# Moving a 56 KB result store from ScalarE's queue amid the loads to SyncE's queue behind the last loads

## Chip, cores, metric

One core of a Trainium2 chip. The metric is the device time of one execution in microseconds (us), the median of several. The kernel before takes 162.1 us.

## The reference

```python
def setup_inputs():
    batch, seq, dim = 32, 512, 1024
    return {"x": np.random.randn(batch, seq, dim).astype(np.float32)}

def reference(x):
    return np.sum(x, axis=-1).astype(np.float32)
```

So 16384 rows of 1024 floats, 67.1 MB read, and 64 KB written. The kernel can hardly be faster than its loads.

## The kernel before

Each of the 128 partitions holds 112 rows of the first block and 16 of the second. Rows come in tiles of 16 a partition (8 MB), three buffers deep, all loaded on SyncE's queue. VectorE sums them; ScalarE helps with seven rows of the last full-width tile and with half of the final block. The final block is loaded in pieces of 9, 4, 2 rows and one row cut at column 544, so that little work is left when the last bytes land. The part that the change touches:

```python
    for b, n in enumerate(BLOCKS):                 # BLOCKS = (112, 16)
        x_b, out_b, res = block(done * P, n)
        ...
        while c < whole:
            ...                                    # loads of 16 rows on nc.sync, sums
            rows_dve(xt, res, 0, m - a, c)
            rows_act(xt, res, m - a, a, c + m - a)
            c += m
        if not final:
            for i, k in ((0, 104), (104, P)):
                nc.scalar.dma_start(out=out_b[i:k], in_=res[i:k])
        done += n

    xt = xpool.tile([P, G * D], F32, tag="xt", name="xt")
    cuts = [0, 9, 13, 15]
    for i, k in zip(cuts, cuts[1:]):
        nc.sync.dma_start(out=xt[:, i * D : k * D], in_=x_b[:, (c + i) * D : (c + k) * D])
    last = 15 * D
    for i, k in ((0, CUT), (CUT, D)):
        nc.sync.dma_start(...)                     # the last row in two pieces
    ...                                            # sums of the final block, VectorE and ScalarE
    nc.sync.dma_start(out=out_b, in_=res)          # the final store, 16 columns
```

Of the kernel before, what the change touches and what calls it, by code (L numbers as in the profile page):

```python
# [1 line left out]

# [4 lines left out]

F32 = mybir.dt.float32
ADD = mybir.AluOpType.add
COPY = mybir.ActivationFunctionType.Copy  # L10
X = mybir.AxisListType.X

BLOCKS = (112, 16)
G = 16
ACT_ROWS = 7
CUT = 544
EARLY = 2


@with_exitstack  # L20
def row_sums(
    ctx: ExitStack,
    tc: tile.TileContext,
    x: bass.AP,
    out: bass.AP,
):
    nc = tc.nc
    P = nc.NUM_PARTITIONS

    x_flat = x.flatten_outer_dims()  # L30
    R, D = x_flat.shape
    C = R // P
    assert R % P == 0 and sum(BLOCKS) == C
    out_flat = out.rearrange("a (b c) -> (a b c)", c=1)

    xpool = ctx.enter_context(tc.tile_pool(name="x", bufs=3))
    rpool = ctx.enter_context(tc.tile_pool(name="res", bufs=1))
    part = rpool.tile([P, 1], F32, name="part")
    seen = rpool.tile([P, 1], F32, name="seen")
    pairs = [rpool.tile([P, D // 2], F32, name=f"pairs{i}") for i in range(3)]  # L40

    def rows_dve(xt, res, j, n, c):
        nc.vector.tensor_reduce(  # L43
            out=res[:, c : c + n],
            in_=xt[:, j * D : (j + n) * D].rearrange("p (j d) -> p j d", d=D),
            axis=X,
            op=ADD,
        )

    def sum_act(v, acc):  # L50
        nc.scalar.activation(out=v, in_=v, func=COPY, accum_out=acc)  # L51

    def rows_act(xt, res, j, n, c):
        for i in range(n):
            sum_act(xt[:, (j + i) * D : (j + i + 1) * D], res[:, c + i : c + i + 1])

    def pairs_dve(xt, a, b, first, acc, pairs):
        h = (a + b) // 2
        nc.vector.tensor_tensor_reduce(  # L59
            out=pairs[:, 0 : h - a], in0=xt[:, a:h], in1=xt[:, h:b], scale=1.0, scalar=first,  # L60
            op0=ADD, op1=ADD, accum_out=acc,
        )

    def block(r0, n):
        x_b = x_flat[r0 : r0 + P * n].rearrange("(p c) d -> p (c d)", p=P)
        out_b = out_flat[r0 : r0 + P * n].rearrange("(p c) -> p c", p=P)
        return x_b, out_b, rpool.tile([P, n], F32, name=f"res{r0}")

    full = C - G
    done = 0  # L70
    for b, n in enumerate(BLOCKS):
        x_b, out_b, res = block(done * P, n)
        final = b == len(BLOCKS) - 1
        whole = n - G if final else n
        c = 0
        while c < whole:
            m = min(G, whole - c)
            xt = xpool.tile([P, G * D], F32, tag="xt", name="xt")
            parts = (0, 1, m) if done + c == 0 else (0, m)
            for i, k in zip(parts, parts[1:]):  # L80
                nc.sync.dma_start(
                    out=xt[:, i * D : k * D], in_=x_b[:, (c + i) * D : (c + k) * D]
                )
            a = ACT_ROWS if done + c + m == full else 0
            rows_dve(xt, res, 0, m - a, c)
            rows_act(xt, res, m - a, a, c + m - a)
            c += m
        if not final:

            for i, k in ((0, 104), (104, P)):  # L90
                nc.scalar.dma_start(out=out_b[i:k], in_=res[i:k])
        done += n

    xt = xpool.tile([P, G * D], F32, tag="xt", name="xt")
# [5 lines that stand above are left out]
        nc.sync.dma_start(  # L100
            out=xt[:, last + i : last + k],
            in_=x_b[:, c * D + last + i : c * D + last + k],
        )

    for i, k in zip(cuts[:2], cuts[1:3]):
        h = (k - i) // 2
        rows_dve(xt, res, i, h, c + i)
        rows_act(xt, res, i + h, k - i - h, c + i + h)
    pairs_dve(xt, 13 * D, 14 * D, 0.0, res[:, c + 13 : c + 14], pairs[2])
    rows_act(xt, res, 14, 1, c + 14)  # L110
    pairs_dve(xt, last, last + CUT, 0.0, part, pairs[0])


    nc.vector.tensor_copy(out=seen, in_=part)  # L114
    pairs_dve(xt, last + CUT, last + D, part, res[:, c + 15 : c + 16], pairs[1])
    nc.sync.dma_start(out=out_b, in_=res)


def kernel(tc: tile.TileContext, x: bass.AP, out: bass.AP):
    row_sums(tc, x, out)  # L120
    tc.close()
    tc.compile()  # L122



    sp = mybir.EngineType.SP
    fn = tc.nc.m.functions[0]
    entry, body = None, None
    for blk in fn.blocks:
        ops = [i for i in blk.instructions if i.engine == sp]  # L130
        if entry is None:
            entry = blk
        elif any(i.opcode == "DMACopy" for i in ops):
            body = blk
            break
    code = list(body.instructions)
    loads = [i for i in code if i.engine == sp][:EARLY]
    for load in loads:
        assert load.opcode == "DMACopy" and not load.sync_info.on_wait
        code.remove(load)  # L140
    body.instructions = code
    code = list(entry.instructions)
    at = next(k for k, i in enumerate(code) if i.engine == sp and i.opcode == "Drain")
    code[at:at] = loads
    entry.instructions = code

# [1 line left out]
_INS = ['x']  # L148
_OUTS = [((32, 512), 'float32')]


# [23 lines left out]
```

## Time and profile before

| | before |
|---|---|
| median time, first 3 runs | 162.1 us (162.03 to 162.14) |
| span of the profiled run | 160.6 us |
| VectorE, ScalarE busy | 76%, 11% of the span |
| load queue (q1) | 97.2% of 16 DMA engines |
| last load piece landed, final store issued, final store landed | 157.80, 158.36, 159.78 us |

Three kinds of reading are used below. The page gives shares. The list in order of time gives start and length of each instruction; a wait stands in brackets behind it. And the trace also keeps a record of each DMA packet (start, length, queue, bytes) and of each semaphore update. Those records do not name the DMA engine, but its packets follow each other end to start within some 5 ns, so an engine can be followed through its long packets. Packet times that no profile line shows are read from those records.

### The profile page before, as it was taken

How to read it: one execution, taken by the hardware profiler on the slowest of the kernel's cores; microseconds unless marked ns; L12 is line 12 of the kernel's file. 1: busy time of each engine (PE TensorE's matmuls, PEld its weight loads, DVE VectorE, ACT ScalarE, POOL GpSimd, SP SyncE). 2: the span in 40 equal slices, each digit the busy share in tenths (PEclk: the TensorE clock that was granted, in tenths of full speed). 3: DMA queues.
4: the chain of work that ended last, by engine and by line, in shares of the span. 5: the costliest groups of instructions: out<-in, count | busy, mean ns of one | idle time of the engine just before them, and what ended most of it. 6: DMA issues, size and time to landing. Idle time of an engine off the chain costs nothing.

```text
span 160.6 us, 120 instructions
## 1 busy us (share of the span) xinstructions
DVE 121.4 (76%) x16; ACT 17.2 (11%) x31; POOL 0.2 (0%) x4
## 2 busy tenths in 40 slices
DVE  0000059997799958999499994999949999598884
ACT  0000000000000000000000000000000000596892
POOL 0000000000000000000000000000000000000000
DMA  9997996996996996996996979979969969998991
GB/s 375 490 398 337 490 522 294 490 522 261 522 506 278 522 506 278 522 506 278 522 506 278 522 326 457 522 310 473 522 294 490 522 261 522 432 432 369 410 402 62
DMA packets 2169, 67.18 MB, mean 418 GB/s; under 512 B 505, under 2 KB 633, under 8 KB 889
## 3 DMA queue, kind: packets, MB, share of 16 engines
q1 hardware_dynamic: 2016, 67.12, 97.2%
q10 hardware_dynamic: 153, 0.06, 0.1%
HBM read 67.11 MB, written 0.07 MB: 418 GB/s over the span
## 4 chain that ended last, share of the span: by engine, by line
DMA 75%; DVE 22%; SPq 0%; issue 0%; DVEq 0%
DMA xt<-in_x_dram 75%; DVE res L43 21%; DVE pairs L59 1%; SPq L97 0%; DVE seen L114 0%; DVE part L59 0%; DVEq L122 0%; DVE res L59 0%
## 5 line engine op out<-in xcount | busy, mean ns | idle before, releaser
L43 DVE TENSOR_REDUCE res<-xt 128x16 f32<-128x16384 f32 (+3 forms) x9 | 119.8, 13309 | 36.6 <-DMA xt<-in_x_dram 36.6
L51 ACT ACT_TABLE_LOAD x1 | 1.3, 1283 | 138.3 <-DMA xt<-in_x_dram 138.3
L51 ACT ACTIVATE xt<-xt 128x1024 f32<-128x1024 f32 x15 | 15.6, 1042 | 2.2 <-DMA xt<-in_x_dram 2.2
L51 ACT ACTIVATION_READ_ACCUMULATOR xt<-xt 128x1 f32 x15 | 2.8, 186 | 0.0
L59 DVE CUSTOM_DVE_ANT_0 pairs<-xt 128x512 f32<-128x512 f32 (+1 forms) x2 | 1.1, 566 | 0.3 <-DMA xt<-in_x_dram 0.3
L59 DVE CUSTOM_DVE_ANT_0 pairs<-xt,part 128x240 f32<-128x240 f32 x1 | 0.5, 467 | 0.0
L114 DVE COPY seen<-part 128x1 f32<-128x1 f32 x1 | 0.2, 153 | 0.0
L59 DVE DVE_READ_ACCUMULATOR2_ANT res<- 128x1 f32 x2 | 0.2, 81 | 0.0
L159 POOL MEMSET const-bfloat16-1.0<- 128x1 bf16 x1 | 0.1, 101 | 0.0
L159 POOL MEMSET const-uint8-127<- 128x1 uint8 x1 | 0.1, 101 | 0.0
L159 POOL MEMSET const-float32-0.0<- 128x1 f32 x1 | 0.1, 98 | 0.2 <-issue 0.2
L159 POOL MEMSET const-float32-1.0<- 128x1 f32 x1 | 0.1, 98 | 0.0
L59 DVE DVE_READ_ACCUMULATOR2_ANT part<- 128x1 f32 x1 | 0.1, 84 | 0.0
## 6 DMA issues: line engine op xcount, KB each, us to landing
xt<-in_x_dram SPq DMA_DIRECT2D x1, 7680.0 KB
xt<-in_x_dram SPq DMA_DIRECT2D x1, 4608.0 KB, 32.4
xt<-in_x_dram SPq DMA_DIRECT2D x1, 2048.0 KB, 36.9
xt<-in_x_dram SPq DMA_DIRECT2D x1, 1024.0 KB, 39.0
xt<-in_x_dram SPq DMA_DIRECT2D x1, 512.0 KB, 3.9
xt<-in_x_dram SPq DMA_DIRECT2D x1, 272.0 KB, 39.1
xt<-in_x_dram SPq DMA_DIRECT2D x1, 240.0 KB, 38.9
xt<-in_x_dram SPq DMA_DIRECT2D x6, 40.9
```

The lines of the kernel that those rows point to most:

```text
L43: nc.vector.tensor_reduce(out=res[:, c : c + n], in_=xt[:, j * D : (j + n) * D].rearrange("p (j d) -> p j d", d=D), axis=X, op=ADD,)
L51: nc.scalar.activation(out=v, in_=v, func=COPY, accum_out=acc)
L59: nc.vector.tensor_tensor_reduce(out=pairs[:, 0 : h - a], in0=xt[:, a:h], in1=xt[:, h:b], scale=1.0, scalar=first, op0=ADD, op1=ADD, accum ...
L114: nc.vector.tensor_copy(out=seen, in_=part)
L159: nc = _bacc.Bacc("TRN2", target_bir_lowering=False, num_devices=1)
```

## The change

The intent: keep the store's packets out of the way of the last loads, by queuing them behind these on the same queue, so that they run while VectorE finishes the last sums.

```diff
         if not final:
-            for i, k in ((0, 104), (104, P)):
-                nc.scalar.dma_start(out=out_b[i:k], in_=res[i:k])
+            out_a, res_a = out_b, res
         done += n
 ...
+    for i, k in ((0, 64), (64, P)):              # behind the loads of the final block
+        nc.sync.dma_start(out=out_a[i:k], in_=res_a[i:k])
```

Three things change at once: the queue, the place behind the loads, and the split.

## The prediction

> **What bounds the kernel now.** I read the page of the profile first (busy shares, chain that ended last), then the chain in order of time, the order-of-time list of the last microseconds, and then the DMA queues in narrow stretches around the moment when the store moves. From the page and its DMA part:
>
> ```profile
> span 160.6 us, 120 instructions
> DVE 121.4 (76%) x16; ACT 17.2 (11%) x31; POOL 0.2 (0%) x4
> DMA packets 2169, 67.18 MB, mean 418 GB/s; under 512 B 505, under 2 KB 633, under 8 KB 889
> q1 hardware_dynamic: 2016, 67.12, 97.2%
> q10 hardware_dynamic: 153, 0.06, 0.1%
> DMA 75%; DVE 22%; SPq 0%; issue 0%; DVEq 0%
> ```
>
> The reader should see that the load queue (q1, SyncE's) fills 97.2% of the time of 16 DMA engines, while VectorE is busy for 76% and ScalarE for 11%. The kernel reads 67.11 MB and the DMA engines are never idle until the end; the chain's 22% on VectorE is time in which loads run beside it (it holds a buffer, the next loads are already queued). So the time is: start-up, the stream of loads, and a short tail after the last bytes land. Only these can change it. ScalarE's queue (q10, which carries the store that the change moves) has 0.1%.
>
> The tail, from the list in order of time of the last four microseconds:
>
> ```profile
> 156.62 0.69 DVE L59 CUSTOM_DVE_ANT_0 pairs<-xt 128x512 f32<-128x512 f32 x1 [0.26 <-DMA xt<-in_x_dram]
> 157.24 0.44 DVE L59 CUSTOM_DVE_ANT_0 pairs<-xt 128x272 f32<-128x272 f32 x1
> 157.73 0.15 DVE L114 COPY seen<-part 128x1 f32<-128x1 f32 x1
> 157.82 0.47 DVE L59 CUSTOM_DVE_ANT_0 pairs<-xt,part 128x240 f32<-128x240 f32 x1
> 158.36 0.35 SPq L116 DMA_DIRECT2D out_dram<-res  x1
> ```
>
> Columns: start, length, engine, line, operation. The last three load pieces land, VectorE adds each as it comes, and at 158.36 SyncE issues the 8 KB store of the last 16 columns. By the trace's semaphore records the last load piece (480 columns) gets its sixteenth and last update at 157.80, and the last VectorE sum starts at 157.82: landing and VectorE's own sequence meet there within some 0.1 us. The final store lands at 159.78 and the rest to 160.6 is the closing of the program.
>
> Where the moved store stands now: ScalarE's own list, and the DMA queues from 148 to 151.8 us and from 151.8 to 155.95 us:
>
> ```profile
> 146.83 0.18 ACT L51 ACTIVATION_READ_ACCUMULATOR xt<-xt 128x1 f32 x1
> 148.11 0.98 ACTq L91 DMA_DIRECT2D out_dram<-res  x2
> 149.20 1.06 ACT L51 ACTIVATE xt<-xt 128x1024 f32<-128x1024 f32 x1 [2.19 <-DMA xt<-in_x_dram]
> ```
>
> ```profile
> q1 hardware_dynamic: 111, 1.56, 95.7%
> ```
>
> ```profile
> q1 hardware_dynamic: 201, 1.62, 92.3%
> q10 hardware_dynamic: 149, 0.06, 5.1%
> ```
>
> The store's two parts (104 and 24 partitions) are issued at 148.11 and done being issued at 149.09, but none of their packets runs before 151.86; then they run in the gaps of the loads until about 155.7 (5.1% of engine time in that stretch, with their few semaphore packets).
>
> **What the Trainium skill says.** On "DMA: Bandwidth & Descriptors", section "Why a DMA increments its semaphore by 16 and not by 1", the number of DMA engines used is the largest number up to 16 that divides the slowest dimension, and each adds a semaphore packet: 104 partitions give 13 engines, 24 give 12, 64 give 16. The trace agrees: 128 rows + 13 + 12 = 153 packets on q10. Its section "Issuing engines are not separate DMA queues" says that DMAs of all issuing engines run on the same 16 DMA engines and interleave; the stretch above shows q10 and q1 side by side. "Queues, rings and completion order" says that each DMA engine consumes one queue's descriptors in ring order and alternates between queues packet by packet; in the single packet records the store rows indeed stand one by one between load packets. And "Anatomy of one DMA" (on the software path, but it names the cause as general) puts most of the fixed cost on the receipt of the last write; here the final store's last packet ends at 159.41 and its last semaphore update is at 159.78, so 0.37 us.
>
> **The change part by part.**
>
> *Removed: two issues on ScalarE.* 0.98 us of ScalarE's sequencer, 148.11 to 149.09. ScalarE's next instruction waits for the 9-row load, which has its last update at 149.16. Gain on the path: 0. ScalarE's last sum ends at 157.78, and the final store waits for VectorE until 158.3 anyway.
>
> *Removed: store packets amid the loads.* In the packet records a 448 B row takes 25 ns, and a 16 KB load packet behind which a row slipped in starts its successor 628 ns later in place of 607: 21 ns each. A DMA engine of the 13 carries 8 rows of the first part, and 12 of them also 2 of the second: 8 to 10 times 21 ns is 0.17 to 0.21 us, with its semaphore packets at most 0.24 us. But three of the sixteen engines carry none, and the slowest engine is one of those: its last 16 KB packet ends at 153.63, the next engines' at 153.52 and 153.40, and it took no row. At the very end the last load packets of the engines end at 157.38 (that engine), then 157.32, 157.31, 157.30. A load counts as landed when all sixteen engines have reported, so the slowest engine sets it. The split into 104 and 24 has placed the cost on engines that had slack. Taking it away brings the other engines forward by about 0.2 us and the landing by some 0.0 to 0.05 us.
>
> *Added: two issues on SyncE.* By the built program the first waits for the column sums (VectorE done at 148.02), the second also for the semaphore of the sixth full-width load, long landed. SyncE has issued its last load by 119.24 and then only waits for the final sum, so about 1 us of issuing from 148.1 to 149.1 lies in idle time: 0.
>
> *Moved: the packets.* Each DMA engine gets 4 rows of each half plus a semaphore packet for each, 10 packets at up to 25 ns: 0.2 to 0.25 us behind its last load packet. From 157.38 that ends at about 157.6; plus the 0.37 us of receipt, 158.0. The final store's issue is at 158.36, and its packets started 0.84 us later (159.20). So the moved store runs in a stretch (157.4 to 159.2) where the DMA engines are idle now, and lands 1.7 us before the store that ends the program. On the path: 0.
>
> *Sum:* 0 - (0.00 to 0.05) + 0 + 0 us. From 162.1 this gives about 162.05, and I say 162.0 since a little variation in which DMA engine is slowest favours the kernel without store packets: in executions where a store-carrying engine is slowest, the gain could be up to 0.2 us.
>
> **The rivals.**
>
> *A, the store packets are on the path.* Then the loads end 0.2 us sooner and the time becomes about 161.9. For it: the end times of the sixteen engines lie within 0.1 us or so of each other at the top (157.38, 157.32), so the store has eaten nearly all the slack. Against it: the slowest engine carries none, and VectorE's last three operations follow each other with almost no gap, so a landing that comes 0.1 us sooner would find VectorE still at the copy.
>
> *B, the store at the end delays the final store.* It stands in the same queue, before it. If its rows were slow to write (each under 512 B) or were fetched late, the final store's packets would queue: 0.2 us for the same time again, perhaps 0.5 us if the final landing must wait for earlier writes: 162.3 to 162.6. Against it: 1.6 us between the last load packet and the final store's first packet, for 0.25 us of work.
>
> *C, a new wait on SyncE.* If the issue of a half blocked SyncE until the loads had drained (a queue that is full), the final store's issue could slip. Against it: SyncE issued five loads in a row from 116.80 to 119.24 while full-width loads were in flight. At 148.1 fewer loads are outstanding. If it happened it would cost up to 1 us: 163.
>
> *D, ScalarE starts earlier on the last block.* It waits for the landing either way, so nothing.
>
> **Range and chances.** The three runs before lie within 0.11 us (162.03 to 162.14). My estimate 162.0 us; A pulls to 161.8 at the best, B to 162.5. I take 161.7 to 162.4. A change of 2% is 3.2 us, more than any rival makes: faster 1%, same 98%, slower 1%.
>
> **What would show it.** Right: no q10 in the profile; q1 with 2016 + 128 + 32 = 2176 packets and 512 under 512 B (505 - 25 + 32); no store packets before about 157; the 448 B packets between 157.1 and 157.7; the last load piece landing within 0.1 us of now relative to its start of the stream; the final store still issued about 0.5 us after that landing and landing 1.4 us after issue; ScalarE's first sum of the last block still started by a landing. Wrong: the last load piece landing 0.2 us or more earlier and VectorE following it (A); a final store of more than 1.6 us from issue to landing (B); a SyncE issue of a half longer than 1 us (C). And if the load stream itself ran at a different rate, none of my parts would cover it.

## The result

| | before | changed |
|---|---|---|
| median, 6 runs each of the same job | 162.13 us (162.03 to 162.42) | 162.38 us (162.17 to 162.40) |
| median of a second job, 9 and 5 runs | 162.22 us (162.12 to 162.59) | 162.19 us (162.06 to 162.33) |

The ratio, the mean of the changed kernel's fast runs over the mean of the other's fast runs of the same rounds (so not quite the ratio of these medians), was 1.001 (95% interval 0.9997 to 1.0023) in the first job and 0.9997 (0.9983 to 1.001) in the second. No difference is shown: the same.

Read first which part of the profile did change. From the page of the changed kernel:

```profile
span 160.4 us, 121 instructions
DVE 121.5 (76%) x16; ACT 17.1 (11%) x31; POOL 0.2 (0%) x4
DMA packets 2176, 67.18 MB, mean 419 GB/s; under 512 B 512, under 2 KB 640, under 8 KB 896
q1 hardware_dynamic: 2176, 67.18, 97.4%
```

ScalarE's queue q10 is gone, and q1 has exactly the 2176 packets, 512 of them under 512 bytes, that the prediction counted. Now the list in order of time around the issue of the store and at the end:

```profile
147.82 1.16 SPq L106 DMA_DIRECT2D out_dram<-res  x2
148.96 1.06 ACT L51 ACTIVATE xt<-xt 128x1024 f32<-128x1024 f32 x1 [2.22 <-issue]
...
156.29 0.69 DVE L59 CUSTOM_DVE_ANT_0 pairs<-xt 128x512 f32<-128x512 f32 x1 [0.20 <-DMA xt<-in_x_dram]
156.98 0.44 DVE L59 CUSTOM_DVE_ANT_0 pairs<-xt 128x272 f32<-128x272 f32 x1
157.47 0.15 DVE L117 COPY seen<-part 128x1 f32<-128x1 f32 x1
157.60 0.47 DVE L59 CUSTOM_DVE_ANT_0 pairs<-xt,part 128x240 f32<-128x240 f32 x1
158.14 0.35 SPq L119 DMA_DIRECT2D out_dram<-res  x1
```

The two issues take SyncE 1.16 us from 147.82, in time when it has nothing else to do. ScalarE's first sum of the final block still starts at the landing of its load (148.89 by the semaphore record, 148.96 by the list); "issue" in the bracket only says that its several waits were already over by this profile. The last four lines are 0.2 to 0.3 us earlier than before, and the last load piece landed at 157.57 in place of 157.80. That looks like a gain, and by the letter it is the prediction's sign of rival A. It is none: the 9-row load already ended 0.30 us earlier, before the store came into play, as the next table shows.

The store's rows ran from 156.44 to 157.27, on each DMA engine behind that engine's own last load packet; the slowest engine's came at 157.09. Their two semaphores were complete at 157.76 and 157.94, before the final store was even issued (158.14). DMA issues with their time from issue to landing, in the changed kernel:

```profile
out_dram<-res SPq DMA_DIRECT2D x2, 28.0 KB, 9.7
out_dram<-res SPq DMA_DIRECT2D x1, 8.0 KB, 1.4
```

The 9.7 us of the moved store are time behind the loads and hurt nobody. The final store needs 1.4 us as before.

### The profile page after: what moved, and what is told of

It is laid out like the page before. It is cut to its first block, busy times and chain, and to the rows that moved or that the text cites. A ratio compares the mean times of both kernels' runs of the same rounds, so it can differ in the third digit from the quotient of the medians.

```text
span 160.4 us, 121 instructions
## 1 busy us (share of the span) xinstructions
DVE 121.5 (76%) x16; ACT 17.1 (11%) x31; POOL 0.2 (0%) x4
## 2 busy tenths in 40 slices
DMA packets 2176, 67.18 MB, mean 419 GB/s; under 512 B 512, under 2 KB 640, under 8 KB 896
## 3 DMA queue, kind: packets, MB, share of 16 engines
q1 hardware_dynamic: 2176, 67.18, 97.4%
## 4 chain that ended last, share of the span: by engine, by line
DMA 75%; DVE 23%; SPq 0%; issue 0%; DVEq 0%
DMA xt<-in_x_dram 75%; DVE res L43 21%; DVE pairs L59 1%; SPq L95 0%; DVE seen L117 0%; DVE part L59 0%; DVEq L125 0%; DVE res L59 0%
```

## How to compare traces that differ by less than their noise

Single runs of one kernel scatter by up to 0.5 us here, more than the 0.2 us that rival A gives the store. So I took a ruler out of the packet records that begins where the stream's earlier scatter is over: the *loads' tail*, from the end of the last 36,864-byte packet (the 9-row load, on the DMA engine that is then last) to the end of the very last load packet. It holds only 16 KB, 8 KB, 2 KB packets of the final block and whatever slips in between. Beside it stands the *lag*, from the last load packet to the load's sixteenth semaphore update.

```
kernel                   9-row load's   last load   loads'   lag     final store's
                         last packet    packet      tail     (us)    issue to landing
before                   148.77         157.38      8.61     0.43    1.42
changed                  148.47         157.09      8.62     0.49    1.43
changed, second job      148.34         157.00      8.67     0.49    1.42
no store at all          148.60         157.27      8.67     0.42    1.42
SyncE, 104 and 24        148.53         157.13      8.61     0.38    1.42
ScalarE, one of 128      148.88         157.66      8.78     0.31    1.42
ScalarE, 64 and 64       148.61         157.40      8.79     0.39    1.41
ScalarE, 128, once more  148.85         157.63      8.78     0.31    1.42
ScalarE, 127 and 1       148.41         157.39      8.99     0.36    2.32
ScalarE, pieces          148.69         157.53      8.84     1.32    1.42
SyncE, pieces            148.72         157.39      8.67     0.89    2.26
SyncE, amid the loads    148.34         159.10     10.76     0.35    1.42
```

The first column, in which the store has no part yet in any of these kernels, differs by 0.54 us between traces. From there to the end of the program the eight traces that have no store, or whole 448-byte rows spread over the engines (all but the one amid the loads on SyncE), take 11.78 to 12.03 us, which differs by 0.25. So more of the scatter comes from the stream's start and middle than from the stretch that the store touches. Each kernel has one trace, the changed one two, whose tails differ by 0.05: smaller differences in this table say nothing.

## The experiments

Each run goes against the kernel before on the same chip. "ScalarE" variants start from the kernel before, "SyncE" variants from the changed one.

### 1. The changed kernel again

No edit, more rounds.

> The changed kernel once more, with more rounds, since its median stood 0.25 us above that of before and the interval included zero. Theory (the moved store lies in a stretch where the DMA engines are idle and costs nothing): median within 0.1 us of the kernel before, and from the landing of the last full-width tile to the start of the final store's issue 20.1 to 20.2 us, as in both traces so far (20.11 before, 20.17 after). Rival (the rows behind the last loads delay the landing of the last load piece or the final store): 0.15 to 0.3 us above before in every round, with the interval clear of zero.

162.19 us against 162.22 of before; ratio 0.9997. From the landing of the last full-width tile to the final issue it took 20.20 us, as expected, and its loads' tail is among those without rows in the way. The 0.25 us between the medians of the first job were not found again. The rival, 0.15 to 0.3 us in every round, is not met.

### 2. No store of the first 112 columns (wrong on purpose)

```diff
-    for i, k in ((0, 64), (64, P)):
-        nc.sync.dma_start(out=out_a[i:k], in_=res_a[i:k])
```

> Wrong on purpose: the first 112 columns are never stored, so this is the floor under both placements. Theory: the store costs nothing in the changed kernel and at most 0.05 us in the kernel before, so this run is within 0.1 us of before. Rival A (the store rows amid the loads are on the path of the kernel before): 0.2 us below before. Rival B (the rows behind the loads cost): below the changed kernel by 0.15 to 0.3 us.

162.47 us against 162.22, ratio 1.0013 (1.0000 to 1.0025): if anything above, by more than the 0.1 us that I allowed. A kernel that does strictly less was not faster, so this measures the noise of such comparisons and not a cost; by time alone, then, two kernels some 0.2 us apart can't be told from equal ones here. The finer ruler agrees: its tail is 8.67 us, against 8.61 and 8.62 to 8.67 with the store at either place. The floor under both placements is not below either of them within what can be measured, and neither rival, which wanted 0.15 to 0.3 us less, is seen.

### 3. and 4. Amid the loads, but on all sixteen DMA engines

```diff
-            for i, k in ((0, 104), (104, P)):
-                nc.scalar.dma_start(out=out_b[i:k], in_=res[i:k])
+            nc.scalar.dma_start(out=out_b, in_=res)            # run 3
+            for i, k in ((0, 64), (64, P)): ...                # run 4
```

> The kernel before with its store as one transfer of 128 partitions on ScalarE's queue amid the loads: 8 rows on each of the 16 DMA engines, so also on the slowest. Theory (only the slowest engine counts): the last load piece lands 8 x 21 ns = 0.17 us later against the landing of the last full-width tile, and the time is 0.1 to 0.2 us above before. Rival (which engines carry the rows makes no difference, the whole is hidden or shared): same as before within 0.05 us.

> The kernel before with the split alone changed to 64 and 64 partitions, still on ScalarE's queue amid the loads: 4 + 4 rows and two semaphore packets on each of the 16 DMA engines. Theory: as the transfer in one piece, 0.1 to 0.25 us above before. With it the change is taken apart: split alone here, place and queue in the changed kernel. Rival: same as before within 0.05 us.

162.39 and 162.34 us against 162.22: ratios 1.0008 (0.9995 to 1.0021) and 1.0004 (0.9992 to 1.0017). The times don't decide, but the traces do: tails of 8.78 and 8.79 us, where the kernels without rows on the slowest engine have 8.61 to 8.67. That is 0.11 to 0.18 us, next to the 0.17 us of 8 rows at 21 ns. The DMA part of run 3 between 151 and 156 us:

```profile
q1 hardware_dynamic: 263, 1.97, 93.0%
q10 hardware_dynamic: 144, 0.06, 4.2%
```

All 128 rows and 16 semaphore packets of q10 are here between load packets. So rows amid the loads do cost, once each of the engines carries some, and in its trace the 104-and-24 split of the kernel before avoids it. That the slowest engine is one without rows is seen in that one trace; whether it is so in every execution the records, which don't name engines, can't tell.

### 5. All rows on one DMA engine

```diff
-            for i, k in ((0, 104), (104, P)):
+            for i, k in ((0, 127), (127, P)):
```

> The kernel before with its split changed from 104 and 24 partitions to 127 and 1, on ScalarE's queue amid the loads: as many rows as before, but all on one DMA engine, since 127 has no divisor up to 16 but 1. Theory (a load has landed when the last of the sixteen engines has, so the distribution counts and not the number): one row slips in per load packet, some 26 of them before the loads end, 0.5 us on that engine, which becomes the slowest: loads' tail 8.8 to 9.1 us in place of 8.6 to 8.7; the other hundred rows follow behind the loads at 25 ns each, to about 160 us, and the end waits for them: time 0.6 to 1.2 us above before. Rival (only the number of rows counts, shared by all engines): within 0.2 us of before.

163.25 us against 162.21, ratio 1.0069 (1.0052 to 1.0086): 1.04 us more, and a tail of 8.99 us, both inside what the theory gave. The total number of rows is the same as before, only their distribution is not. First the page, then the DMA part from 157.5 us to the end, with the final store's landing:

```profile
q10 hardware_dynamic: 130, 0.06, 0.1%
```

```profile
q10 hardware_dynamic: 96, 0.04, 2.9%
out_dram<-res SPq DMA_DIRECT2D x1, 8.0 KB, 2.3
```

130 packets are 128 rows and two semaphore packets, one engine for each transfer. 30 rows got in before the last load packet ended at 157.39 (I expected 26), one per load packet; the rest run after the loads, the last until 159.68, and the final store, whose own rows on that engine wait among them, lands 2.3 us after issue in place of 1.4. The number of rows is unchanged and the time is not: what counts is the last of the sixteen DMA engines.

### 6. Many more packets, amid the loads

The same bytes in 7 pieces of 15 columns and 7 of 1 column a partition:

```diff
+            o7 = out_b.rearrange("p (a b) -> p a b", b=16)
+            r7 = res.rearrange("p (a b) -> p a b", b=16)
+            for i, k in ((0, 15), (15, 16)):
+                nc.scalar.dma_start(out=o7[:, :, i:k], in_=r7[:, :, i:k])
```

> The cost made larger: the same bytes of the same store, on ScalarE's queue amid the loads, but in 7 pieces of 60 bytes and 7 of 4 bytes a partition, so 112 packets on every DMA engine in place of 8 to 10 on thirteen. Theory (rows amid the loads delay each engine that carries them, the slowest too): at 10 to 21 ns each the loads' tail (from the slowest engine's last 9-row packet to the last load packet, 8.61 us before) grows by 1.1 to 2.4 us, and so does the time. Rival (rows amid the loads are hidden): tail and time unchanged. A caveat: ScalarE has 0.1 us to spare at the issue and some 0.5 us at the end; should issuing so many pieces take it more than 0.6 us longer, its sums become the end, and the last load packet is then the thing to read, not the time.

163.19 us against 162.19, ratio 1.0056 (1.0039 to 1.0073): 1.0 us more, a little under the expected 1.1 to 2.4, and not by the expected way. The tail grew only to 8.84 us. What grew is the lag. VectorE's last sum, which had not waited, now does:

```profile
157.23 0.44 DVE L59 CUSTOM_DVE_ANT_0 pairs<-xt 128x272 f32<-128x272 f32 x1
...
157.71 0.15 DVE L116 COPY seen<-part 128x1 f32<-128x1 f32 x1
158.88 0.47 DVE L59 CUSTOM_DVE_ANT_0 pairs<-xt,part 128x240 f32<-128x240 f32 x1 [1.02 <-DMA xt<-in_x_dram]
```

Its load's last packet ended at 157.53, its last semaphore update came at 158.86, 1.32 us later in place of 0.43. Ten of the load's sixteen engines had reported by 157.57, the other six between 158.06 and 158.86, and VectorE started only after the last. Only about one piece got in for each load packet: by 157.1, 498 of the 1824 packets of q10 had run, none of them a 60-byte piece (the one-column transfer was issued first, at 146.84). The others ran when the engines were coming to the end of their loads or were done. As a test of rows *amid* the loads the run is a failure: most of its pieces were not amid them. What it shows is that, with this crowd of small writes, the report of a load that has already been moved comes late.

### 7. Many more packets, behind the loads

The same pieces with `nc.sync` in the changed kernel.

> The same 112 packets on every DMA engine, on SyncE's queue behind the last loads. Theory (the stretch between the last load packet and the final store's first packet, some 1.9 us, is free): the loads' tail stays at 8.6 to 8.7 us; the pieces take 1.1 to 2.4 us, so at the upper end they push the final store by up to 0.5 us; the time is 0 to 0.5 us above before, and well below that of the same pieces amid the loads. Rival B (rows behind the loads delay the final store by their whole length): 1.1 to 2.4 us above before, as much as amid the loads.

163.71 us against 162.19, ratio 1.0092 (1.0077 to 1.0107): 1.5 us more. The theory gave 0 to 0.5 and less than amid the loads; it is more. Rival B's size was met, but not its way. The list in order of time:

```profile
147.98 5.84 SPq L108 DMA_DIRECT2D out_dram<-res  x2
...
158.30 0.47 DVE L59 CUSTOM_DVE_ANT_0 pairs<-xt,part 128x240 f32<-128x240 f32 x1 [0.51 <-DMA xt<-in_x_dram]
...
158.84 0.35 SPq L121 DMA_DIRECT2D out_dram<-res  x1
```

The final store among the DMA issues (KB, us to landing):

```profile
out_dram<-res SPq DMA_DIRECT2D x1, 8.0 KB, 2.3
```

And SyncE's own waits (us in total, times, longest), where its wait for stores at the end was 0.8 us in both kernels compared:

```profile
SPq L127 <- DMA out_dram<-res: 1.6, 2, 1.4
```

The tail is 8.67 us: behind the loads the pieces don't slow the loads' packets, as the theory says. But three things stand against it. The lag is 0.89 us in place of 0.4, so VectorE waits 0.51 us; it is one report of the sixteen, at 158.28, where the other fifteen had come by 157.75. The final store lands 2.26 us after issue in place of 1.42. And the one-column pieces report last at 160.94, 2.8 us after the last of their packets at 158.13. Against the changed kernel's trace (final landing 159.57, here 161.10) that is: stream later by 0.25 at the start of the tail, tail 0.05, lag 0.40, final store 0.83, together 1.53 us. So "the stretch behind the loads is free" is true for 8 rows an engine and false for 112 tiny pieces. I had counted the time of packets and not that of their reports.

The issue of the two took SyncE 5.84 us, the second alone 5.12 us by its record and the first, with as many pieces, 0.62. In run 6 the same two transfers took ScalarE 0.55 and 0.60 us. So it is not the number or the size of the pieces in one transfer; a backlog in the queue fits, but was not tested by itself. A SyncE issue that blocks, rival C of the prediction, does exist, only not at 128 rows.

### 8. On SyncE's queue, but ahead of four of the loads

```diff
     for i, k in zip(cuts, cuts[1:]):
+        if i == 9:
+            nc.sync.dma_start(out=out_a, in_=res_a)
         nc.sync.dma_start(out=xt[...], in_=x_b[...])
 ...
-    for i, k in ((0, 64), (64, P)):
-        nc.sync.dma_start(out=out_a[i:k], in_=res_a[i:k])
```

> The changed kernel with the store placed on SyncE's queue between the 9-row load and the 4-row load instead of behind all loads. Theory: SyncE waits for the column sums until about 147.8 us before it can issue the four loads behind the store, and the DMA engines run out of packets at about 148.5 us; with 0.5 us for the store's issue, 0.4 us for that of the load and some 0.8 us from issue to the first packet, a gap of 0.6 to 1.2 us in the loads and as much in the time. Rival (a store's place on the queue does not matter, since it is small): within 0.2 us of before.

164.08 us against 162.19, ratio 1.0114 (1.0099 to 1.0129): 1.9 us more, in the theory's direction but above its 0.6 to 1.2. Issues in order, and the DMA share (second last column) and GB/s by stretches:

```profile
147.62 0.35 SPq L96 DMA_DIRECT2D out_dram<-res  x1
148.02 0.90 SPq L97 DMA_DIRECT2D xt<-in_x_dram  x2
```

```profile
147.00:148.00 1.00, 0.55 (x1) 0.00 (x0) 0.00 (x0) 1.00 0.00 0
148.00:148.50 0.50, 0.00 (x0) 0.00 (x0) 0.00 (x0) 1.00 0.04 6
148.50:149.00 0.50, 0.29 (x1) 0.24 (x1) 0.00 (x0) 1.00 0.41 109
149.00:149.50 0.50, 0.50 (x1) 0.50 (x1) 0.00 (x0) 1.00 2.54 492
149.50:150.00 0.50, 0.50 (x1) 0.50 (x3) 0.00 (x0) 1.00 0.14 33
```

A packet counts in the stretch in which it starts, so the zero at 147 is made of long packets that had started before. The 9-row load ends at 148.34; the last engine to go on starts its first packet of the next load at 149.58, 1.24 us later, at the upper end of the gap that I had estimated. What I had left out is that the stream then needs time to come up to speed: the first 16 KB packet of each engine takes 0.96 to 1.94 us, where later ones take 0.61. From 149.58 the 4-row load takes to 155.36, 5.78 us, where the same stretch takes 4.86 us in the changed kernel (148.47 to 153.33). 1.24 + 0.92 = 2.16 us is the tail's growth of 2.14. This run also tells why the changed kernel puts its two stores *behind* the loads: SyncE issues in order, and a store that waits for sums blocks every load after it.

### 9. The old split at the new place

```diff
-    for i, k in ((0, 64), (64, P)):
+    for i, k in ((0, 104), (104, P)):
```

> The changed kernel with the split of before (104 and 24 partitions) on SyncE's queue behind the loads: the change of place alone, without that of the split. Theory: behind the loads the split is of no account; loads' tail 8.6 to 8.7 us and time within 0.15 us of before and of the changed kernel. Rival (13 engines in place of 16 matter there too): the final store lands later by up to 0.2 us against the last load piece.

162.18 us against 162.19, ratio 1.0001 (0.9986 to 1.0016); tail 8.61, final store 1.42 us. Behind the loads the split is of no account.

### 10. A third place, which it did not take

```diff
-    for i, k in ((0, 64), (64, P)):
-        nc.sync.dma_start(out=out_a[i:k], in_=res_a[i:k])
 ...
     rows_act(xt, res, 14, 1, c + 14)
+    nc.scalar.dma_start(out=out_a, in_=res_a)
```

> A third place for the store: one transfer of 128 partitions on ScalarE's queue behind ScalarE's own last sum, issued at about 157.6 us, after the last load packet. Theory (the DMA engines are idle from 157.4 to 159.2 us): its rows run at about 158.5 to 158.7 us and land at about 159.1 us, ahead of the final store; loads' tail 8.6 to 8.7 us, landing of the last piece 0.31 to 0.49 us behind its last packet as in the other runs, time within 0.15 us of before. Rival (any rows between the loads and the final store delay it): the final store lands more than 1.55 us after its issue.

162.46 us against 162.21, ratio 1.0015 (1.0000 to 1.0030). The trace has the store's rows between 151.47 and 155.00, not after 157.6: the scheduler placed the issue right behind ScalarE's first seven sums, whatever the order of the source lines. So the run tests nothing of what I wrote; it is run 3 once more, and its tail of 8.78 us is a third sample for that. A store on ScalarE's queue after its last sum stays untried.

## Why the prediction was right

*The bound.* Right. The end of the stream of loads, VectorE's short tail and the final store set the time in every run; ScalarE, 0.98 us of issuing lighter, gave nothing.

*Removed packets: 0.00 to 0.05 us.* Right in kind: with no rows on the slowest engine the tail is 8.61 to 8.67 us over five traces, with rows on every engine 8.78 to 8.79 over three, and with 30 rows on one engine 8.99. In its trace the kernel before had paid for its rows out of other engines' slack. Rival A, 0.2 us, is not met by these tails. How much slack there is differs from trace to trace, though. In that of the kernel before the two slowest engines end the 9-row load at 148.77 and 148.65, and neither carries a row up to the end of its 16 KB packets (both take 4.86 us for them); the third ends at 148.50. In the four others without rows amid the loads the slowest is 0.01 to 0.37 us behind the next. Where that is little, rows worth 0.2 us on the next engine could come onto the path, as the prediction itself allows. That they stayed off it is shown for one execution and not for all.

*Moved packets: 0 on the path.* Right for this store: its semaphores were complete 0.20 us before the final store's issue, and that store still took 1.43 us. But the margin was overstated. The prediction let the store land 0.36 us ahead of the final issue, and compared it with the final landing as if only packets had to fit. It took the 0.37 us from the final store's last packet to its report for the moved store too; there it was 0.67 us (157.27 to 157.94).

Three smaller points of the prediction do not hold. The sign "no store packets before about 157" was missed: the rows ran from 156.44, since the first engine was done with its loads 0.65 us before the slowest. The receipt is not most of the final store's 1.42 us: 0.84 of them lie before its first packet and 0.37 behind its last. And from the last load packet to the final store's first packet (157.38 to 159.20) it is 1.8 us, not the 1.6 that stand under rival B.

Runs 6 and 7 show that small writes around the end of the loads also delay the semaphores of the loads. At 8 rows an engine this is not seen: the changed kernel's two lags of 0.49 us stand against 0.31 to 0.43 of the undisturbed runs, but in the first of them the 2-row load, which landed at 156.27, before the store's first row at 156.44, had 0.48 already. Whether some 0.03 us of it is the rows stays open.

*The lean to 162.0.* Not borne out. I let the missing rows be worth up to 0.1 us on average. The medians are 162.38 and 162.19 in two jobs, with before at 162.13 and 162.22; neither a gain nor a loss is shown. That 162.38 still lies under the range's upper end of 162.4 is luck, since the scatter of the runs is not a term of the sum.

*Rivals C and D.* SyncE's two issues took 1.16 us, in idle time, so C is out for the change; an issue that took microseconds was seen in run 7. ScalarE still waited for its load (D).

## What to carry to other kernels

A load counts as landed when the last of the sixteen DMA engines has reported. So before moving a small store out of a load stream, look whether it stands on the slowest engine: the split of a transfer decides how many engines carry it, and it was worth a microsecond in the wrong direction (127 rows on one) and nothing measurable in the right one. Here the small store behind the last loads was as cheap as the one hidden in slack; it was not once it had 112 pieces an engine (run 7), nor where the loads had to wait for its issue (run 8). And under half a microsecond, compare stretches within traces instead of medians.

## What the Trainium skill lacked or had wrong

- "DMA: Bandwidth & Descriptors", "Queues, rings and completion order", gives some 9 to 17 descriptors as the typical packet that an engine drains from one queue before it turns to another. Here one 448-byte row went in per load packet: 30 rows on one engine between 151.7 and 157.4 us, and 8 rows of the kernel before spread over 3.9 us.
- The same section says that a semaphore increment lands only after every earlier write of that DMA engine, over its queues. That fits run 6, where the small writes were another queue's. It doesn't tell that writes queued *behind* the load delay its report too: the lag was 0.89 us in run 7 (one of the sixteen reports), against 0.31 to 0.49 in all runs with 448-byte rows or no store. Which writes hold it back, those of the same engine or the crowd at the memory, is open.
- No page gives what a stream of loads loses when it runs dry: in run 8 it was 1.24 us of gap and 0.92 us until it was at speed again.
- No page gives what a small store's row costs the stream that it interrupts: 21 ns on the engine that carries it, 0.11 to 0.18 us for 8 rows.
